# A decoder layer on one core: the third merge gate by seven products, spread over the branch pieces, and x's factor copied before x is scaled

## The chip, the core and the metric

The kernel runs on one core of a Trainium2 chip. Its engines are TensorE (PE in the profile, with PEld for its weight loads), VectorE (DVE), ScalarE (ACT), GpSimd (POOL) and SyncE (SP). Each takes its instructions in the order in which they were written down when the program was built, and waits on semaphores for the others. The metric is device microseconds of one execution.

## The reference, cut to what matters

```python
h = rms_norm(x, norm_g)                                  # x: 256 tokens x 1024
(qa, ka, va, ga, ub, vb, gb, qc, gc, ma, mb, mc) = split_cols(h @ w_in, IN_SPLITS)
out_a = moba_attention(rope(qa), rope(ka), va) * silu(ga)      # 6 heads of 128
out_b = gmlp_spatial_gate(ub, vb, ...) * silu(gb)              # 6 groups of 128
out_c = memory_cross_attention(qc, rms_norm(mem), ...) * silu(gc)   # 4 heads of 128
y = (sigmoid(ma) * (out_a @ w_branch_a)
     + sigmoid(mb) * (out_b @ w_branch_b)
     + sigmoid(mc) * (out_c @ w_branch_c))
return rms_norm(x + y @ w_out, final_norm_g)
```

All numbers are float32. `ma`, `mb` and `mc`, the arguments of the three merge gates, are each a product of the 256 x 1024 tokens with 1024 x 1024 weights.

## The kernel before, in words

**Three passes for one product.** Every float32 operand is split into a high part, rounded to the format that TensorE takes (`hi`, `nh`, `ah`, ...), and a low part, the rest (`lo`, `nl`, `al`, ...). A product is high times high, high times low, low times high, summed in PSUM: `mm3`, lines 391 to 394. The activations are split once. The weights stream from memory and are split on the way: ACT copies a piece to its high part (`split_hi`, line 232), DVE subtracts for the low part (`split_lo`, line 236).

**Chunks.** The weights come in pieces of 1 MB, 128 rows of 2048 numbers, and a piece is two chunks. The list `chunks` is the program's spine; it is made from `PLAN`, and the main loop goes over it with index `c`. In each round the loop runs the small units that are due, splits chunk `c + LEAD` (LEAD is 3), asks for a later piece, and writes down the matmuls of chunk `c`. There are three buffers for raw pieces and four pairs of `hi` and `lo`. A `fea` chunk gives 128 columns of one projection for all tokens (16 matmuls, line 548). A `tok` chunk gives 512 columns for two of the eight blocks of 128 input rows (12 matmuls, lines 392 to 394). A `br` chunk takes two blocks of 128 rows of the branch weights; the first eight of them make the left half of y, the next eight the right half, each in the order of the branches a, a, a, b, b, b, c, c. An `out` chunk belongs to the last projection.

**Gates by seven products.** The first two merge gates (0 for branch a, 1 for branch b) go by Strassen's scheme in Winograd's form: tokens and input rows are halved, sums of the blocks are formed, and seven block products stand for eight. The tokens' sums are the tile `s` (`sums`, line 444), made once and kept in the slot named `x2`. The weights' sums are formed by DMA: a block is loaded into one of two buffers, `form_510` (slot `f0`) and `form_636` (slot `mr`), and further blocks are added to it by accumulating DMAs, which POOL issues (lines 212 and 215). In the order 1, 2, 5, 3, 6, 7, 4 the first buffer serves products 1, 5, 6 and 4, the second 2, 3 and 7. A product is a piece of two `st` chunks of six matmuls (`mm_st`, line 484). Its result goes to the tile of the gate in part by ACT copies (line 491) and DVE additions (lines 495, 498 and 500). Product 4 runs on in the PSUM bank of product 7, so its first matmul waits for DVE's subtraction c22, line 500. The third gate (2, for branch c) is plain: eight `tok` chunks named `sig`, after everything else of the input projection.

**What sets the order.** The helper `Units` holds all work beside the streaming: attention, norms, joins, gates. Each unit has an engine, an estimated duration, units that must come first, and a due chunk. It writes a unit down when the estimate says that it fits, and at the due chunk in any case. The order on each engine is thus fixed at build time. A chunk's join is an ACT copy (line 556) and a DVE addition (558); `jt` is its tile for the gates. SiLU of branch b's gate (line 597) is followed on POOL by u times that (598) and by the mixed result times that (988); the product is split for the branch matmul (`obh` on ACT at line 958, `obl` on DVE at 962). The sigmoids are at line 503. The last lines before the output are `y_units`: y is transposed on PE and split.

**The head.** The norm of x needs the tokens' factor. PE spreads it over the partitions in PSUM (`rms_bcast`, line 352), DVE multiplies the first four blocks of x by it from there (`norm_k`, line 642), and POOL the other four from a copy in SBUF, `bc`, that ACT makes (`rms_out`, line 357); ACT first scales those four blocks by the norm's gain (`norm_gain`, line 646). DVE's first multiplication waits for the copy `bc`, since both read the same PSUM bank.

Of the kernel before, what the change touches and what calls it, by code (L numbers as in the profile page):

```python
# [46 lines left out]
FAST = 2  # L47


def plan():  # L50
# [16 lines left out]

TOK = ("vvb", "mv", "sig")
# [66 lines left out]
def tile_hybrid_layer(ctx: ExitStack, tc: tile.TileContext, mw, xT, mem, x, fin_g, ln_g, w, ws, w_sp, b_sp, rope, out):  # L135
# [272 lines left out]
    def mm_tok(c):  # L408
# [22 lines left out]
        elif k0 + 2 == KD and name == "sig":  # L431
            g = o // 512
            if g == 4:
                slot_tile("sigc", [128, 2, 2, 512], "p1")
            sig[g] = V["sigc"][:, g - 4]

            for t in range(2):
                nc.scalar.activation(sig[g][:, t, :], acc[name, o][t], AF.Sigmoid)
                U.run(ACT, 0.62, U.end[f"c{c}"])
# [24 lines left out]
    def mm_st(c):  # L464
# [23 lines left out]
        c11, c21, c12, c22 = (sig[2 * g + o][:, t, :] for o in range(2) for t in range(2))  # L488
# [12 lines left out]
        if i == 4:  # L501
# [471 lines left out]
    sig2 = chunks.index(("tok", "sig", 2048, 6))  # L973
    last_st = max(c for c in range(n_in) if chunks[c][0] == "st")
    U.add("oaTa", None, 0, lambda: pair("a", "x2", HA), after=[f"c{last_st}"])
    for i in range(3):
# [3 lines left out]
        two_split(f"oaT{i}", lambda hs=hs: (V["qk"][:, hs, 0, :], V["ah"][:, hs, :], V["al"][:, hs, :]),  # L980
                  [f"ga_{i}", "oaTa"], due=sig2 - 2)
# [13 lines left out]
    for i in range(3):  # L995
        hs = slice(2 * i, 2 * i + 2)
        two_split(f"obT{i}", lambda hs=hs: (V["ub"][:, hs, :], V["obh"][:, hs, :], V["obl"][:, hs, :]),
                  [f"mg{i}", "obTa"])
    for i in range(2):
# [4 lines left out]
                  [f"gc_{i}", "ocTa"])  # L1004
    U.add("fin", None, 0, load_fin, after=["oaT0", "oaT1", "oaT2"], wait=8.0)
# [4 lines left out]
    def y_units(half, i, after):  # L1010
# [102 lines left out]
    for c in range(n_in):  # L1113
# [160 lines left out]
```

## Time and profile before

| what | us |
|---|---|
| median of 3 runs | 324.89 (324.81 to 325.85) |
| the profiled execution, its own time | 325.81 |
| its span, first to last instruction | 324.1 |

| engine | busy us | share of the span |
|---|---|---|
| PE | 314.0 | 97% |
| PEld | 266.8 | 82% |
| DVE | 246.7 | 76% |
| ACT | 212.5 | 66% |
| POOL | 50.1 | 15% |

The profiled execution is 0.92 us longer than the median, and 1.7 us of its time lie outside the span. Matmuls are pipelined, so two that follow each other overlap in the records: what one costs is the distance between starts. TensorE's granted clock is full, 0.998 on average.

### The profile page before, as it was taken

What the parts mean: (1) busy time and instruction counts of PE and PEld (TensorE: products, weight loads), DVE (VectorE), ACT (ScalarE), POOL (GpSimd) and SP (SyncE); (2) the same over time, 40 slices, a digit from 0 to 9 for tenths busy, and PEclk for the clock granted to TensorE, in tenths of its full rate; (3) what the DMA queues carried; (4) which work ended last, traced back from release to release, by engine and by line L of the source; (5) the groups of instructions that cost most, each with busy time, mean ns of one, the idle gap of its engine ahead of it and who ended that gap; (6) DMA issues with size and microseconds to landing.
All of it is one profiled execution on the core that took longest, in us unless ns stands there. A gap on an engine that the chain in (4) does not pass through costs nothing.

```text
span 324.1 us, 4506 instructions
## 1 busy us (share of the span) xinstructions
PE 314.0 (97%) x1638; PEld 266.8 (82%) x1638; DVE 246.7 (76%) x353; ACT 212.5 (66%) x354; POOL 50.1 (15%) x50
## 2 busy tenths in 40 slices
PE   8998999999999999999999999998999999999992
PEld 4886888889888888888888888887888888888982
DVE  3979989597579678869687899879775559769452
ACT  4868785564988566786787796567995633434433
POOL 1004730001001110000300441644310000000022
PEclk9999999999999999999999999999999999999999
DMA  7999796845469899488589789823658466463003
GB/s 247 407 421 358 302 330 242 370 138 163 90 229 261 151 232 302 146 257 325 166 169 358 155 229 250 238 113 129 215 203 290 145 235 275 161 230 130 0 8 124
DMA packets 14422, 71.21 MB, mean 220 GB/s; under 512 B 1856, under 2 KB 3008, under 8 KB 8128
## 3 DMA queue, kind: packets, MB, share of 16 engines
q1 hardware_dynamic: 12960, 62.21, 53.1%
q0 software_dynamic: 1152, 8.39, 13.9%
q10 hardware_dynamic: 288, 0.33, 0.3%
q8 instruction: 13, 0.21, 0.3%
q14 instruction: 9, 0.07, 0.1%
HBM read 69.08 MB, written 1.05 MB: 216 GB/s over the span
## 4 chain that ended last, share of the span: by engine, by line
PE 85%; DMA 7%; ACT 4%; DVE 3%; issue 0%; ACTq 0%; SPq 0%
PE acc L548 31%; PE acc L393 11%; PE acc L394 11%; PE acc L392 11%; PE acc L484 10%; DMA st<-in_mw_dram 3%; DMA xt<-in_xT_dram 3%; PE aux L393 2%; PE aux L394 2%; PE aux L392 2%; DVE lo L236 2%; PE aux L718 2%; ACT hi L232 1%; PE aux L942 1%; DVE n L400 1%; DVE xt L642 1%
## 5 line engine op out<-in xcount | busy, mean ns | idle before, releaser
L236 DVE TENSOR_TENSOR lo<-raw,hi 128x1024 fp32r<-128x1024 f32 x86 | 113.6, 1327 | 41.4 <-ACT hi L232 40.2
L232 ACT ACTIVATE hi<-raw 128x1024 fp32r<-128x1024 f32 x86 | 90.5, 1058 | 37.1 <-PE acc L394 30.8
L548 PE MATMUL acc<-n,hi 128*128 128x512 f32 x304 | 79.9, 393 | 0.0
L548 PEld LDWEIGHTS acc<-n,hi 128*128 128x128 f32 x304 | 55.4, 189 | 9.6
L548 PEld LDWEIGHTS acc<-n,lo 128*128 128x128 f32 x304 | 41.4, 190 | 3.8 <-DVE lo L236 0.8
L548 PE MATMUL acc<-n,lo 128*128 128x256 f32 x304 | 42.5, 282 | 0.4 <-DVE lo L236 0.4
L236 DVE TENSOR_TENSOR lo<-form,hi 128x1024 fp32r<-128x1024 f32 x28 | 35.5, 1280 | 6.0 <-ACT hi L232 6.0
L393 PE MATMUL acc<-lo,n 128*128 128x512 f32 x80 | 31.2, 391 | 1.3 <-DVE lo L236 1.3
L392 PE MATMUL acc<-hi,n 128*128 128x512 f32 x80 | 31.3, 391 | 0.1
L394 PE MATMUL acc<-hi,n 128*128 128x512 f32 x80 | 31.1, 389 | 0.0
L232 ACT ACTIVATE hi<-form 128x1024 fp32r<-128x1024 f32 x28 | 29.2, 1051 | 0.5 <-PE acc L484 0.5
L215 POOL DMA_DIRECT2D form<-in_ws_dram x8 | 7.1, 884 | 135.0 <-DVE lo L236 129.9
L484 PE MATMUL acc<-hi,s 128*128 128x512 f32 x64 | 21.9, 397 | 0.0
L393 PEld LDWEIGHTS acc<-lo,n 128*128 128x128 f32 x80 | 15.0, 188 | 4.6 <-DVE lo L236 1.6
L392 PEld LDWEIGHTS acc<-hi,n 128*128 128x128 f32 x80 | 15.0, 188 | 3.5 <-ACT hi L232 0.4
L394 PEld LDWEIGHTS acc<-hi,n 128*128 128x128 f32 x80 | 15.0, 188 | 3.1
L484 PE MATMUL acc<-hi,n 128*128 128x512 f32 x48 | 16.6, 399 | 1.0 <-ACT obh L958 1.0
L1087 POOL TENSOR_TENSOR xk<-xk,fing 128x512 f32<-128x512 f32 (+1 forms) x4 | 4.0, 1013 | 78.9 <-ACT jk L1083 78.9
L484 PEld LDWEIGHTS acc<-hi,s 128*128 128x128 f32 x64 | 12.0, 188 | 2.3
L484 PE MATMUL acc<-lo,s 128*128 128x512 f32 x32 | 12.5, 391 | 0.0
L556 ACT ACTIVATE qk<-acc 128x256 f32<-128x256 f32 x12 | 4.6, 386 | 11.7 <-PE acc L548 11.7
L556 ACT ACTIVATE jt<-acc 128x256 f32<-128x256 f32 x14 | 5.3, 380 | 10.4 <-PE acc L548 10.3
(227 smaller groups left out, 579.3 us busy)
## 6 DMA issues: line engine op xcount, KB each, us to landing
raw<-in_w_dram SPq DMA_DIRECT2D x34, 1024.0 KB, 4.8
raw<-in_w_dram SPq DMA_DIRECT2D x18, 512.0 KB, 7.8
form<-in_ws_dram POOLq DMA_DIRECT2D x8, 1024.0 KB, 8.4
form<-in_ws_dram SPq DMA_DIRECT2D x6, 1024.0 KB, 5.5
st<-in_mw_dram SPq DMA_DIRECT2D x6, 384.0 KB, 7.1
xk<-in_x_dram SPq DMA_DIRECT2D x2, 512.0 KB, 8.9
xt<-in_xT_dram SPq DMA_DIRECT2D x2, 512.0 KB, 10.1
mm<-in_mem_dram SPq DMA_DIRECT2D x2, 512.0 KB, 11.9
```

The source lines that it names most:

```text
L215: nc.gpsimd.dma_start(form_tile(i), block(g, b), accum_op=OP.add)
L232: nc.scalar.activation(hi[c][:, a:b], raw[c // 2][:, o + a:o + b], AF.Copy)
L236: nc.vector.tensor_tensor(lo[c][:, a:b], raw[c // 2][:, o + a:o + b], hi[c][:, a:b].bitcast(F32), OP.subtract)
L392: nc.tensor.matmul(p, s_hi, m_hi, start=first, stop=False)
L393: nc.tensor.matmul(p, s_hi, m_lo, start=False, stop=False)
L394: nc.tensor.matmul(p, s_lo, m_hi, start=False, stop=last)
L400: nc.vector.tensor_tensor(dl, p, dh.bitcast(F32), OP.subtract)
L484: nc.tensor.matmul(p, x[:, k0 + k, tsl(t)], wt[c][:, a * 512:(a + 1) * 512], start=first and a + j == 0, stop=half == 1 and a + j == 3, sk ...
L548: nc.tensor.matmul(o, wt, m, start=i == 0, stop=i == len(passes) - 1)
L556: nc.scalar.activation(dst, pa, AF.Copy)
L718: nc.tensor.transpose(p[:, hsl(j)], src, ident)
L1087: nc.gpsimd.tensor_tensor(z, z, V["fing"][:, a:b], OP.mult)
```

## The change

- `FAST` is 3: the third gate goes by seven products as well. Its eight `tok` chunks are gone, and 14 `st` chunks come in; its weights lie in memory as blocks for this scheme, with the left and right half of the columns exchanged.
- The first two gates' products are placed so that every two of the last `fea` chunks are followed by one product: the sixth and the seventh product of gate 1 each move ahead by two `fea` chunks.
- The third gate's seven products and the eight branch pieces (two chunks each) are dealt in turn: product, piece, product, piece, and so on, the pieces in the order left a, left a and b, left b, right a, right a and b, right b, and at last left c, right c without a product between.
- The third gate's products use the other four PSUM banks (`aux`); the branch sums keep `acc`. The tokens' sums and the normed tokens must stay until the last product, so branch a's parts `ah` and `al` go to other slots and are split earlier, and y's tile is made after product 4.
- The sigmoids are due when their branch piece needs them, the table of square roots is loaded after the last branch chunk, and the final gain is loaded after the last use of `ah`.
- In the head, `norm_gain` waits for `xrms`, the copy `bc`.

```diff
-FAST = 2
+FAST = 3
...
+    late = st[15:]
+    del st[15:]
...
-                 "ub4", "", "ga0", "", "ga2", "", "ga4", "", "gb0", "gb2", "", "gb4", ""):
+                 "ub4", "", "ga0", "", "ga2", "", "ga4", "", "gb0", "", "gb2", "", "gb4", ""):
...
-    return p + [("sig", g) for g in range(2 * FAST, 6)]
+    br = [("br", (h, i)) for h, i in ((0, 0), (0, 1), (0, 2), (1, 0), (1, 1), (1, 2), (0, 3), (1, 3))]
+    for piece, n in zip(br, (1, 1, 1, 1, 1, 1, 0, 0)):
+        p += [piece] + late[:n]
+        del late[:n]
+    return p
...
-            acc[key] = acc_bank()
+            acc[key] = acc_bank() if g < 2 else bank()
...
+        def gate(o, after, due):
+            y = sig[2 * g + o]
+            U.add(f"sgm{g}{o}", ACT, 1.1, lambda: nc.scalar.activation(y, y, AF.Sigmoid), after=["silu"] + after, due=due)
+
+        if g == 2 and i == 7:
+            gate(0, ["c122", "c222"], at_br[0, 7])
+        elif g == 2 and i == 4:
+            gate(1, ["c112", "p24"], at_br[1, 7])
+            pair("y", "n2", KD)
+        elif i == 4:
             for o in range(2):
-                U.add(f"sgm{g}{o}", ACT, 1.1, lambda o=o: nc.scalar.activation(sig[2 * g + o], sig[2 * g + o], AF.Sigmoid),
-                      after=["silu", f"c11{g}", f"c12{g}", f"c22{g}", f"p{g}4"], due=n_in - 8 + 2 * g + o)
+                gate(o, [f"c11{g}", f"c12{g}", f"c22{g}", f"p{g}4"], at_br[o, 2 + 3 * g] - o)
...
-            U.add(f"ng{k}", ACT, 0.42, lambda k=k: norm_gain(k), after=["load_xt"], due=5)
+            U.add(f"ng{k}", ACT, 0.42, lambda k=k: norm_gain(k), after=["load_xt", "xrms"], due=6)
...
-    U.add("oaTa", None, 0, lambda: pair("a", "x2", HA), after=[f"c{last_st}"])
+    def alloc_a():
+        slot_tile("ah", [128, HA, S], "ga", F32R)
+        low = slot_tile("al0", [128, 4, S], "gc", F32R), slot_tile("al1", [128, 2, S], "v1", F32R)
+        V["al"] = [low[0][:, 0:2, :], low[0][:, 2:4, :], low[1]]
...
-                  [f"ga_{i}", "oaTa"], due=sig2 - 2)
+                  [f"ga_{i}", "oaTa"], due=at_br[0, i] - 2)
...
-    U.add("fin", None, 0, load_fin, after=["oaT0", "oaT1", "oaT2"], wait=8.0)
+    U.add("fin", None, 0, load_fin, after=[f"c{at_br[1, 2]}"], wait=8.0)
...
-        if half == 0 and part == 0:
-            nc.scalar.preload_act_table(AF.Sqrt)
-            pair("y", "n2", KD)
...
-                    y_units(half, i, [f"y{c}"])
+                    y_units(half, i, [f"y{c}", f"c{last_st}"])
```

The changed file's line numbers are a few higher or lower for the same code: its `split_hi` is line 238, `split_lo` 242, the product's matmul 482, the join 562 and 564.

**In the head, ACT.** The rows after the second pair of weight splits, before and then changed; `jt` is a join of the memory's keys, `xt` the tokens, `bc` the copy of the factor, `n` the normed tokens' high part.

```order
L232 ACTIVATE hi<-raw 128x1024 x2
L556 ACTIVATE jt<-acc 128x256
L646 ACTIVATE xt<-xt,gains 128x256 x4
L357 ACTIVATE bc<-aux 128x256
L651 ACTIVATE n<-xt 128x2x256 x2
```

```order
L238 ACTIVATE hi<-raw 128x1024 x2
L562 ACTIVATE jt<-acc 128x256
L363 ACTIVATE bc<-aux 128x256
L652 ACTIVATE xt<-xt,gains 128x256 x4
L657 ACTIVATE n<-xt 128x2x256 x2
```

The copy `bc` stands ahead of the four scalings.

**Ahead of product 4 of gate 1, DVE.** The rows that end with the subtraction c22 for which product 4's first matmul waits (line 500, then 498; `sigb` and `sigs_1726` are the same gate's tile). `form_510` is the first weight buffer, here with product 4's sum; `al` is branch a's low part.

```order
L558 TENSOR_TENSOR jt<-jt,acc 128x256
L236 TENSOR_TENSOR lo<-raw,hi 128x1024
L962 TENSOR_TENSOR obl<-ub,obh 128x512
L236 TENSOR_TENSOR lo<-form_510,hi 128x1024 x2
L558 TENSOR_TENSOR jt<-jt,acc 128x256
L500 TENSOR_TENSOR sigb<-sigb,acc 128x512
```

```order
L242 TENSOR_TENSOR lo<-raw,hi 128x1024
L564 TENSOR_TENSOR jt<-jt,acc 128x256
L968 TENSOR_TENSOR al_2200<-qk,ah 128x512
L242 TENSOR_TENSOR lo<-raw,hi 128x1024
L242 TENSOR_TENSOR lo<-form_510,hi 128x1024 x2
L564 TENSOR_TENSOR jt<-jt,acc 128x256
L498 TENSOR_TENSOR sigs_1726<-sigs_1726,acc 128x512
```

A low part of branch a has come in where one of branch b's stood, and the rows belong to earlier chunks: before, the join ahead of the subtraction is that of the fifth of the six `gb` chunks, now that of the third.

**Around the first sigmoids, ACT.** Before, these are the rows from the copy of gate 1's last product on. In the changed kernel they are those from the copy of the third gate's product 1 on, while PE goes through product 1, the first branch piece and product 2; there `form_636` and `form_510` are products 2 and 5, the first `raw` row is the second piece's first chunk, the one behind the sigmoids its second chunk.

```order
L491 ACTIVATE sigb<-acc 128x512
L958 ACTIVATE a<-qk 128x2x256 x3
L232 ACTIVATE hi<-raw 128x1024
L597 ACTIVATE jt<-jt 128x512
L232 ACTIVATE hi<-raw 128x1024
L503 ACT_TABLE_LOAD
L503 ACTIVATE sig_858<-sig_858 128x1024
L503 ACTIVATE sig_859<-sig_859 128x1024
L503 ACTIVATE sigb<-sigb 128x1024
L232 ACTIVATE hi<-raw 128x1024
```

```order
L489 ACTIVATE sigs_2389<-aux 128x512
L603 ACTIVATE jt<-jt 128x512
L238 ACTIVATE hi<-form_636 128x1024
L238 ACTIVATE hi<-raw 128x1024
L964 ACTIVATE obh<-ub 128x512
L501 ACT_TABLE_LOAD
L501 ACTIVATE sig_858<-sig_858 128x1024
L501 ACTIVATE sig_859<-sig_859 128x1024
L501 ACTIVATE sigs_1726<-sigs_1726 128x1024
L238 ACTIVATE hi<-raw 128x1024
L238 ACTIVATE hi<-form_510 128x1024 x2
```

The last high part of branch b, `obh`, which waits for POOL, now stands right ahead of the table load and three sigmoids, and a branch chunk's split behind them.

## Rows read from the trace of the kernel before

**Rows 1.** The page's engine table: busy time, share of the span, instructions.

```profile
PE 314.0 (97%) x1638; PEld 266.8 (82%) x1638; DVE 246.7 (76%) x353; ACT 212.5 (66%) x354; POOL 50.1 (15%) x50
```

**Rows 2.** The waits of PE's matmuls: who waited for whom, us in total, times, longest.

```profile
PE acc L393 <- DVE lo L236: 1.3, 1, 1.3
PE acc L484 <- ACT obh L958: 1.0, 1, 1.0
PE acc L548 <- DVE lo L236: 0.4, 1, 0.4
```

**Rows 3.** The third gate's plain product: the group of its first passes from 228.4 to 250.2 us (those of lines 393 and 394 have the same count), then from PE's timeline its first matmul and the first of the branches (start us, us).

```profile
L392 PE MATMUL acc<-hi,n 128*128 128x512 f32 x32 | 12.4, 389 | 0.0
...
228.40 0.39 PE L392 MATMUL acc<-hi,n 128*128 128x512 f32 x1
...
250.16 0.39 PE L392 MATMUL acc<-hi,a 128*128 128x512 f32 x1
```

**Rows 4.** PE's timeline over one product of 12 matmuls (product 7 of gate 1): its first row, and the first row behind it.

```profile
216.10 0.40 PE L484 MATMUL acc<-hi,s 128*128 128x512 f32 x1
...
218.84 1.75 PE L548 MATMUL acc<-n,hi 128*128 128x512 f32 x7
```

**Rows 5.** The timeline of the head, all engines (start us, us, engine, line; in brackets the idle time before and its releaser).

```profile
21.15 0.36 ACT L556 ACTIVATE jt<-acc 128x256 f32<-128x256 f32 x1
21.23 0.40 PE L352 MATMUL aux<-dg,ones 128*128 128x256 f32 x2
22.66 1.71 ACT L646 ACTIVATE xt<-xt,gains 128x256 f32<-128x256 f32 x4 [1.14 <-DMA xt<-in_xT_dram]
22.96 0.41 DVE L558 TENSOR_TENSOR jt<-jt,acc 128x256 f32<-128x256 f32 x1
24.27 0.36 ACT L357 ACTIVATE bc<-aux 128x256 f32<-128x256 f32 x1
24.67 1.66 DVE L642 SCALAR_TENSOR_TENSOR xt<-xt,gains,aux 128x256 f32<-128x256 f32 x4 [1.30 <-ACT bc L357]
26.90 0.36 ACT L556 ACTIVATE jt<-acc 128x256 f32<-128x256 f32 x1
27.16 1.99 ACT L232 ACTIVATE hi<-raw 128x1024 fp32r<-128x1024 f32 x2
28.80 2.35 DVE L236 TENSOR_TENSOR lo<-raw,hi 128x1024 fp32r<-128x1024 f32 x2
30.06 0.50 PE L393 MATMUL acc<-lo,n 128*128 128x512 f32 x1 [1.30 <-DVE lo L236]
```

**Rows 6.** The timeline ahead of product 4 of gate 1: POOL, DVE and PE.

```profile
219.60 1.58 POOL L598 TENSOR_TENSOR ub<-ub,jt 128x512 f32<-128x512 f32 x1 [1.26 <-ACT jt L597]
221.26 2.17 POOL L988 TENSOR_TENSOR ub<-ub,mt 128x512 f32<-128x512 f32 x1
...
220.50 4.01 DVE L236 TENSOR_TENSOR lo<-form,hi 128x1024 fp32r<-128x1024 f32 x2 [0.48 <-ACT hi L232]
224.44 0.41 DVE L558 TENSOR_TENSOR jt<-jt,acc 128x256 f32<-128x256 f32 x1
224.77 0.67 DVE L500 TENSOR_TENSOR sigb<-sigb,acc 128x512 f32<-128x512 f32 x1
...
225.59 0.47 PE L484 MATMUL acc<-hi,n 128*128 128x512 f32 x1 [1.02 <-ACT obh L958]
```

**Rows 7.** The timeline of ACT and POOL around the sigmoids.

```profile
228.60 0.60 ACT L491 ACTIVATE sigb<-acc 128x512 f32<-128x512 f32 x1 [0.29 <-PE acc L484]
231.60 0.62 ACT L597 ACTIVATE jt<-jt 128x512 f32<-128x512 f32 x1
...
232.30 1.81 POOL L598 TENSOR_TENSOR ub<-ub,jt 128x512 f32<-128x512 f32 x1 [8.87 <-ACT jt L597]
234.18 1.64 POOL L988 TENSOR_TENSOR ub<-ub,mt 128x512 f32<-128x512 f32 x1
...
233.19 1.28 ACT L503 ACT_TABLE_LOAD   x1
234.48 2.01 ACT L503 ACTIVATE sig<-sig 128x1024 f32<-128x1024 f32 x2
237.35 1.04 ACT L232 ACTIVATE hi<-raw 128x1024 fp32r<-128x1024 f32 x1
```

**Rows 8.** DVE and POOL side by side, where POOL multiplies branch c by its gate.

```profile
190.34 4.42 DVE L236 TENSOR_TENSOR lo<-raw,hi 128x1024 fp32r<-128x1024 f32 x1
...
190.84 2.83 POOL L953 TENSOR_TENSOR mid<-mid,gc 128x512 f32<-128x512 f32 x2
```

**Rows 9.** From the views of lines 212 and 215: time from issue to landing of the loads of a weight block (six, issued by SP), and below of the accumulating ones (eight, issued by POOL).

```profile
DMA to landing us min/median/max: 4.8/5.5/8.3
...
DMA to landing us min/median/max: 8.2/8.4/10.9
```

**Rows 10.** Busy time of each engine (instructions) in two stretches: the third gate's plain product, and the branches.

```profile
228.40:250.20 21.80, 21.80 (x98) 18.06 (x97) 15.71 (x14) 17.68 (x22) 3.44 (x2) 1.00 0.71 242
250.20:293.70 43.50, 43.50 (x197) 36.09 (x196) 29.98 (x34) 20.32 (x23) 0.00 (x0) 1.00 0.57 205
```

More of the change, by code (lines that the diff above doesn't have):

```diff
@@ L174, in tile_hybrid_layer @@
             chunks += [("tok", name, g * 512, 2 * i) for i in range(4)]
-        elif name == "st":
-            chunks += [("st", *g, i) for i in range(2)]
+        elif name in ("st", "br"):
+            if name == "br" and ("br", 0, 0) not in chunks:
+                n_in = len(chunks)
+            chunks += [("st", *g, i) if name == "st" else ("br", g[0], 2 * g[1] + i) for i in range(2)]
         else:
             chunks.append(("fea", name, g))
-    n_in = len(chunks)
-    for half in range(2):
-        chunks += [("br", half, i) for i in range(KD)]
     n_br = len(chunks)
+    at_br = {k[1:]: i for i, k in enumerate(chunks) if k[0] == "br"}
     for kh in range(2):
@@ L430, in mm_tok @@
             evict_v(c, o)
[L431 to L439, printed above, removed]
         elif k0 + 2 == KD:
@@ L478, in mm_st @@
             else:
-                slot_tile("sigb", [128, 2, 2, 512], "p2")
-                sig[2], sig[3] = (V["sigb"][:, o] for o in range(2))
+                t2 = slot_tile(f"sigs{g}", [128, 2, 2, 512], ("p2", "p1")[g - 1])
+                for o in range(2):
+                    sig[2 * g + o] = t2[:, o]
         for a in range(2):
@@ L487, in mm_st @@
             return
-        c11, c21, c12, c22 = (sig[2 * g + o][:, t, :] for o in range(2) for t in range(2))
+        c11, c21, c12, c22 = (sig[2 * g + o][:, t, :] for o in ((0, 1) if g < 2 else (1, 0)) for t in range(2))
         if i in (1, 5, 6, 4):
@@ L970, in alloc @@
         return fn
-    sig2 = chunks.index(("tok", "sig", 2048, 6))
-    last_st = max(c for c in range(n_in) if chunks[c][0] == "st")
-    U.add("oaTa", None, 0, lambda: pair("a", "x2", HA), after=[f"c{last_st}"])
+    def alloc_a():
+        slot_tile("ah", [128, HA, S], "ga", F32R)
+        low = slot_tile("al0", [128, 4, S], "gc", F32R), slot_tile("al1", [128, 2, S], "v1", F32R)
+        V["al"] = [low[0][:, 0:2, :], low[0][:, 2:4, :], low[1]]
+    U.add("oaTa", None, 0, alloc_a, after=["ga_0", "ga_1", "ga_2", "gc_0", "gc_1", f"av{HA - 1}"])
+    last_st = max(c for c in range(n_br) if chunks[c][0] == "st")
     for i in range(3):
@@ L1019, in turn @@
             U.run(DVE, 0.7, U.run(ACT, 0.62, U.t[PE]))
-        U.add(f"yt{half}{i}", PE, 0.44, turn, after=after)
+        U.add(f"yt{half}{i}", PE, 0.44, turn, after=after, due=10 ** 6 if half else at_br[1, 6])
     def mm_br(c):
         _, half, part = chunks[c]
-        if half == 0 and part == 0:
-            nc.scalar.preload_act_table(AF.Sqrt)
-            pair("y", "n2", KD)
-        src = {"a": (V["ah"], V["al"], HA, 0), "b": (V["obh"], V["obl"], GB, 2),
+        src = {"a": (V["ah"], None, HA, 0), "b": (V["obh"], V["obl"], GB, 2),
                "c": (V["och"], V["ocl"], HC, 4)}
@@ L1035, in mm_br @@
             for t in range(2):
-                mm3(acc[br][t], sh[:, k, tsl(t)], sl[:, k, tsl(t)], hi[c][:, i * 512:(i + 1) * 512],
+                low = sl[:, k, tsl(t)] if sl is not None else V["al"][k // 2][:, k % 2, tsl(t)]
+                mm3(acc[br][t], sh[:, k, tsl(t)], low, hi[c][:, i * 512:(i + 1) * 512],
                     lo[c][:, i * 512:(i + 1) * 512], k == 0, k == n - 1)
@@ L1112, in tile_hybrid_layer @@
     dma, ready, free = {}, {}, [13, 19]
-    for c in range(n_in):
+    for c in range(n_br):
         if chunks[c][0] == "st" and chunks[c][3] == 0:
@@ L1228 @@
             continue
-        if name in TOK:
+        if name == "br":
+            parts.append(br[g].reshape(-1))
+        elif name in TOK:
             parts.append(tok(cols[name][:, g * 512:(g + 1) * 512]))
```

18 lines of the change are left out of this document (9 added, 9 removed).

## The prediction, made before the changed kernel had run

> **What bounds the kernel now.** I read the engine table first: PE is busy 314.0 of 324.1 us, DVE 246.7 [rows 1]. A busy PE is not yet the bound, so I read next what its matmuls waited for: three waits above noise, 1.3, 1.0 and 0.4 us [rows 2]. PE is therefore the bound from the head on; a matmul less saves its time, and everything else counts only where it makes PE wait. The timelines at the first two waits [rows 5, 6] and the order of the instructions then show what comes late there, and what will.
>
> **The change part by part.**
>
> *Matmuls.* The plain product is 3 x 32 = 96 matmuls, from 228.40 to 250.16: 21.76 us, 0.227 each [rows 3]. Seven products are 84. Twelve such matmuls took 218.84 - 216.10 = 2.74, or 0.228 each [rows 4], so 84 take 19.18. Saved: 2.6 us, all on PE. The lower bound is nothing less, since no matmul is added elsewhere.
>
> *Splits.* 14 half-size steps stand for 8 chunks, so ACT gets six more copies of 1.04 [rows 7] and DVE six more subtractions of 2.35 / 2 = 1.18 [rows 5], plus three additions of about 0.67 [rows 6]; two of the four eviction copies replace sigmoids of the same size. For DVE this is 9 us more over the two stretches, in which it now works 15.7 + 30.0 of 65.3 us [rows 10]; 55 of 62.7 is 87%. That is cover while chunks are split three ahead of PE. It ends where ACT or DVE stands still for longer than the lead, which the last item looks for. I cost the splits themselves at nothing.
>
> *Head.* Now DVE's first scaling waits until 24.67 for `bc`, which stands behind ACT's four scalings, which wait for x until 22.66 [rows 5]. PE's spread is over at 21.63, ACT's join at 21.51, so in the new order `bc` is done near 22.0. DVE is free at 22.96 + 0.41 = 23.37 and starts 1.3 earlier. Not all of this reaches PE. The subtraction that PE waits for (28.80) needs the high part, which ACT starts at 27.16 behind a join at 26.90 that is tied to PE; its first copy ends near 28.2. So the subtraction starts at 28.2 and PE goes on at about 29.45 for 30.06: 0.6 saved. Bounds: 0 (another wait ends there) and 1.3 (the whole wait). I take 0.6, since the 27.16 is a row.
>
> *Ahead of product 4 of gate 1.* PE waited 1.02 there, until DVE's c22 was done at 224.77 + 0.67 = 225.44 [rows 6]; the profile names ACT, but the matmul waits for c22 and for a high part. In the new order the product comes after two `gb` chunks as before, and DVE's list ahead of c22 is other. Count from the end of the second `gb` chunk, g. ACT's split for the third chunk comes first, then DVE's: subtraction done at g + 1.6, join 2.0, low part of branch a 2.6, three subtractions 3.8, 4.9, 6.0, join 6.4, c22 at g + 7.1, if POOL were silent. But POOL's two multiplications fall into it (SiLU of the first pair is done near g + 2.7). In [rows 6] two subtractions beside such a pair took 4.01 instead of 2 x 1.18, 1.7 more; so c22 ends near g + 8.8. PE arrives at g + 2.74 + 2 x 2.8 = g + 8.3 (two `fea` chunks behind the product). The wait shrinks from 1.0 to about 0.5: 0.5 saved. Bounds: 1.0 saved (POOL costs nothing), 0.9 lost (POOL's whole pair, as [rows 8] would have it, 3.2).
>
> *The sigmoids (a new wait).* Let E be the end of product 1 of the third gate on PE. ACT's list from there: eviction copy at E + 0.2, SiLU of the last pair until E + 1.3, and POOL's two multiplications from E + 1.4. From SiLU's start to the second one's end it was 235.82 - 231.60 = 4.22 [rows 7], so they end at E + 4.9. ACT meanwhile splits two chunks and then stands at `obh`, which waits for POOL: E + 5.0 to 5.6. Behind it stand the table load (1.28), three sigmoids (2.01 for two, so 1.0 each) and only then the copy for the second chunk of the second branch piece: it starts near E + 9.8, ends at 10.8, and DVE's subtraction at 12.1. PE needs that low part at E + 5.45 (a piece) + 2.74 (product 2) + 2.72 + 0.23 = E + 11.1. PE waits about 1.0; with ACT up to 0.7 late from the weight block before, 1.7. I take 1.2; bounds 0 (sigmoids and POOL each a little faster) and 2.0. Queued behind the copy on ACT are product 5's two splits and one more sigmoid, which PE reaches after E + 13.6; by the same count they are ready in time, and DVE regains its lead in the next piece.
>
> *At nothing.* The adding DMAs: from one use of the first buffer to the next lie 13.65 us of PE (a piece, a product, a piece), the add lands in 8.4, at most 10.9 [rows 9]. The adds stand in POOL's queue, but the gate's multiplications behind them wait later for ACT. On SP the final gain waits for branch a's last matmul; the raw loads behind it wait for splits of later chunks anyway. Transposes of y: DVE's four operations need 2.7 us and a branch chunk lies between. The table of square roots (1.28) sits on ACT two chunks before its splits are needed. Both ends are unchanged.
>
> Sum: -2.6 - 0.6 - 0.5 + 1.2 = -2.5 us. The profiled execution took 325.81, which would become 323.3; the median is 0.92 below it, 324.89, so 322.4.
>
> **A rule of the Trainium skill against it.** In [rows 8] one subtraction lasted 4.42 beside 2.83 of POOL, 3.2 more than its 1.18, almost as if it had stood still; in [rows 6] it lost 1.7 beside 3.83. SBUF — State Buffer, "Who interferes with whom", says that VectorE with two inputs in SBUF and GpSimd reading SBUF exclude each other: whoever comes second stands still until the first is done. The first row agrees, the second only half. By the rule DVE would lose the whole of POOL's pair each time; what that gives is the second rival.
>
> **Rivals.**
> 1. *The waits vanish.* The head gives its whole 1.3, c22 is early (1.0 saved), and the sigmoids end before PE needs the copy: -2.6 - 1.3 - 1.0 = -4.9, 320.0. For it: each of the three misses by about 1 us or less. Against: all three must turn out well.
> 2. *POOL holds DVE out.* The wait ahead of product 4 grows to 1.9 (POOL's pair costs 3.2 as in [rows 8]; 0.9 lost) and the new wait to 1.55 (POOL's own pair took 3.83 in [rows 6] against 3.5): -2.6 - 0.6 + 0.9 + 1.55 = -0.75, 324.1, not to be told from before. For it: [rows 8]. Against: [rows 6], where the same kinds of instruction met.
> 3. *The first block of the third gate comes late: slower.* The first buffer is free when product 4 of gate 1 is split, near g + 7.8 with POOL's share, and product 1 of the third gate follows only two `fea` chunks behind product 4 (before, the nearest such reload had four). After landing it takes 2.4 us to a low part; PE arrives at g + 8.8 + 2.74 + 5.6 = g + 17.1, or 17.3 for the low part. The load may take 6.8 us; six loads took 4.8 to 8.3, median 5.5 [rows 9]. At 8.3 PE waits 1.5, and the change still gains 1.0. From 9.3 it gains nothing; at 10.9, the slowest time of the adds, PE waits 4.1: +1.6, 326.5.
> 4. *The product does not do what it says*, that is, DVE at 87% and not PE sets the pace in the branches. The time would be near 324 as well; I count it with rival 2.
>
> **How the numbers follow.** My forecast, 321.4 to 323.4 by the two small terms, has 0.66; rival 1 0.13; rivals 2 and 4 0.14; rival 3 0.07. The bounds of the unknown costs give 320.0 (all at the good end) to 324.89 - 2.6 + 0.9 + 2.0 = 325.2. I leave out half of rival 1 and rival 3: 320.3 to 324.4. A measurement of this kernel tells about 0.3%, 1.0 us, from no change. Faster is the forecast and rival 1: 0.79; the same is rivals 2 and 4: 0.14; slower is rival 3: 0.07.
>
> **What would show it.** Matmuls of the seven-product line: 252 of them, 0.228 apart; the lines of three passes 96 fewer. In the head `bc` near 22.0, DVE's scaling near 23.4, PE's first low pass near 29.4. Ahead of product 4 of gate 1 a wait of 0.5, released by DVE's c22. In the second branch piece, at its second chunk, PE waits about 1 us for a subtraction whose copy stands behind three sigmoids and a table load. If this wait is missing, the sigmoid term was wrong; if PE waits at product 1 of the third gate or ACT stands there for a DMA, it is rival 3; if many short waits for DVE line up through the branches, it is rival 4.

## The result and the profile after

The changed kernel took 321.62 us (median of 4 runs, 321.49 to 322.15); the kernel before, run beside it, 324.85 (324.56 to 325.85). The ratio is 0.9898 with a 95% interval of 0.9874 to 0.9922: 3.2 us faster, where the prediction said 322.4 and so 2.5 faster. The profiled execution took 321.63, with a span of 319.9 against 324.1: 4.2 less, since the profiled execution of before lay 0.9 above its median.

The engine table, which answers to [rows 1], and PE's waits (us in total, times, longest), which answer to [rows 2]:

```profile
PE 310.6 (97%) x1626; PEld 263.9 (82%) x1626; DVE 251.9 (79%) x362; ACT 220.9 (69%) x362; POOL 54.8 (17%) x54
```

```profile
PE aux L428 <- ACT hi L385: 1.0, 2, 0.8
...
PE acc L482 <- DVE sigs L498: 0.7, 1, 0.7
PE acc L399 <- DVE lo L242: 0.7, 2, 0.5
```

PE has 12 matmuls fewer and ACT and DVE 8 and 9 instructions more, as the splits were counted. In [rows 2] the head's wait was 1.3; it is the small one of the two on line 399 now. The other one on that line, and product 4's on line 482, are the two places that the prediction named. Those on line 428 lie before 8.5 us, long before x comes.

The head's timeline (start us, us, engine, line; in brackets the idle time before and its releaser), beside [rows 5]:

```profile
21.80 0.39 ACT L363 ACTIVATE bc<-aux 128x256 f32<-128x256 f32 x1 [0.19 <-PE aux L358]
22.77 1.71 ACT L652 ACTIVATE xt<-xt,gains 128x256 f32<-128x256 f32 x4 [0.59 <-DMA xt<-in_xT_dram]
25.60 0.37 ACT L562 ACTIVATE jt<-acc 128x256 f32<-128x256 f32 x1
25.87 2.00 ACT L238 ACTIVATE hi<-raw 128x1024 fp32r<-128x1024 f32 x2
...
28.72 0.50 PE L399 MATMUL acc<-lo,n 128*128 128x512 f32 x1 [0.19 <-DVE lo L242]
```

The copy `bc` is done at 22.2, before x comes, and everything behind it moved as one piece: the join from 26.90 to 25.60, the weight copies from 27.16 to 25.87, PE's first low pass from 30.06 to 28.72. That is 1.34, where the prediction had 0.6. What held the join before is shown by the two rows of ACT just ahead of it in the kernel before:

```profile
25.58 0.63 ACT L651 ACTIVATE n<-xt 128x512 fp32r<-128x512 f32 x1 [0.94 <-DVE xt L642]
...
26.36 0.64 ACT L651 ACTIVATE n<-xt 128x512 fp32r<-128x512 f32 x1 [0.15 <-DVE xt L642]
```

Two copies of the normed tokens waited for DVE; the join at 26.90 follows the second without a wait of its own.

Ahead of product 4 of gate 1, beside [rows 6]:

```profile
211.16 2.15 POOL L604 TENSOR_TENSOR ub<-ub,jt 128x512 f32<-128x512 f32 x1 [5.46 <-ACT jt L603]
213.39 2.15 POOL L998 TENSOR_TENSOR ub<-ub,mt 128x512 f32<-128x512 f32 x1
...
212.07 4.55 DVE L242 TENSOR_TENSOR lo<-form,hi 128x1024 fp32r<-128x1024 f32 x2
216.88 0.67 DVE L498 TENSOR_TENSOR sigs<-sigs,acc 128x512 f32<-128x512 f32 x1
...
216.61 0.39 PE L554 MATMUL acc<-n,hi 128*128 128x512 f32 x1
217.70 0.47 PE L482 MATMUL acc<-hi,n 128*128 128x512 f32 x1 [0.70 <-DVE sigs L498]
```

The two subtractions beside POOL's pair took 4.55, c22 ended at 217.55, and PE, there at 217.00, waited 0.70.

Around the first sigmoids, beside [rows 7], with the second branch piece on PE:

```profile
231.79 1.62 POOL L998 TENSOR_TENSOR ub<-ub,mt 128x512 f32<-128x512 f32 x1
...
233.44 0.63 ACT L964 ACTIVATE obh<-ub 128x512 fp32r<-128x512 f32 x1 [0.56 <-POOL ub L998]
234.07 1.28 ACT L501 ACT_TABLE_LOAD   x1
235.37 2.01 ACT L501 ACTIVATE sig<-sig 128x1024 f32<-128x1024 f32 x2
237.28 1.04 ACT L501 ACTIVATE sigs<-sigs 128x1024 f32<-128x1024 f32 x1
238.23 1.05 ACT L238 ACTIVATE hi<-raw 128x1024 fp32r<-128x1024 f32 x1
...
239.31 1.23 DVE L242 TENSOR_TENSOR lo<-raw,hi 128x1024 fp32r<-128x1024 f32 x1 [2.48 <-ACT hi L238]
...
239.73 0.39 PE L398 MATMUL acc<-hi,obh 128*128 128x512 f32 x1
240.59 0.50 PE L399 MATMUL acc<-lo,obh 128*128 128x512 f32 x1 [0.47 <-DVE lo L242]
```

The chain is the foretold one: POOL, `obh`, table, three sigmoids, the copy, the subtraction, PE. The wait is 0.47, not 1.2.

A wait costs PE more than the idle time in its row, since matmuls that don't wait overlap and start 0.23 apart. From start to start it was 1.09 ahead of product 4 (216.61 to 217.70) and 0.86 here, and the next matmul came another 0.1 late: 0.9 and 0.7 us for the 0.70 and 0.47 in the rows.

The seven-product line on PE, beside [rows 4], over product 2 of the third gate:

```profile
234.29 0.39 PE L482 MATMUL aux<-hi,n 128*128 128x512 f32 x1
...
237.01 0.39 PE L398 MATMUL acc<-hi,ah 128*128 128x512 f32 x1
```

Twelve matmuls took 2.72, 0.227 each. The terms as these rows have them, waits counted from start to start: matmuls -2.6, head -1.34, product 4's wait -0.3, the new wait +0.7, and the wait of 0.4 on line 548 [rows 2], which is absent here, -0.6 (start to start 0.80 for 0.23). Their sum, -4.1, is the difference of the two spans to 0.1. The last term isn't the change's (see the end), and without it the sum is -3.5.

### The profile page after: what moved, and what is told of

Read it like the earlier page. It is cut to its first block, busy times and chain, and to the rows that moved or that the text cites. A ratio compares the mean times of both kernels' runs of the same rounds, so it can differ in the third digit from the quotient of the medians.

```text
span 319.9 us, 4510 instructions
## 1 busy us (share of the span) xinstructions
PE 310.6 (97%) x1626; PEld 263.9 (82%) x1626; DVE 251.9 (79%) x362; ACT 220.9 (69%) x362; POOL 54.8 (17%) x54
## 3 DMA queue, kind: packets, MB, share of 16 engines
HBM read 72.23 MB, written 1.05 MB: 229 GB/s over the span
## 4 chain that ended last, share of the span: by engine, by line
PE 82%; DMA 5%; DVE 5%; ACT 3%; issue 3%; POOL 1%; SPq 0%; ACTq 0%; DVEq 0%
PE acc L554 31%; PE acc L482 11%; PE acc L399 8%; PE acc L400 8%; PE acc L398 8%; PE aux L482 5%; DMA xk<-in_x_dram 3%; PE aux L399 2%; PE aux L398 2%; PE aux L400 2%; DVE lo L242 2%; DMA st<-in_mw_dram 2%; PE aux L724 2%; PE aux L948 1%; ACT hi L238 1%
## 5 line engine op out<-in xcount | busy, mean ns | idle before, releaser
L242 DVE TENSOR_TENSOR lo<-raw,hi 128x1024 fp32r<-128x1024 f32 x78 | 99.2, 1283 | 32.1 <-ACT hi L238 30.8
L238 ACT ACTIVATE hi<-raw 128x1024 fp32r<-128x1024 f32 x78 | 82.0, 1058 | 24.4 <-PE acc L400 18.4
L242 DVE TENSOR_TENSOR lo<-form,hi 128x1024 fp32r<-128x1024 f32 x42 | 55.5, 1336 | 9.6 <-ACT hi L238 9.3
L238 ACT ACTIVATE hi<-form 128x1024 fp32r<-128x1024 f32 x42 | 43.9, 1053 | 4.2 <-DMA form<-in_ws_dram 1.9
L221 POOL DMA_DIRECT2D form<-in_ws_dram x12 | 10.6, 883 | 158.4 <-DVE lo L242 152.6
L399 PE MATMUL acc<-lo,n 128*128 128x512 f32 x48 | 18.8, 392 | 0.2 <-DVE lo L242 0.2
L398 PE MATMUL acc<-hi,n 128*128 128x512 f32 x48 | 18.7, 390 | 0.0
L400 PE MATMUL acc<-hi,n 128*128 128x512 f32 x48 | 18.7, 389 | 0.0
L482 PE MATMUL acc<-hi,n 128*128 128x512 f32 x48 | 16.6, 400 | 0.7 <-DVE sigs L498 0.7
L482 PEld LDWEIGHTS acc<-hi,n 128*128 128x128 f32 x48 | 9.0, 188 | 2.7 <-ACT jt L562 1.0
L399 PEld LDWEIGHTS acc<-lo,n 128*128 128x128 f32 x48 | 9.0, 188 | 2.4 <-DVE lo L242 0.6
L400 PEld LDWEIGHTS acc<-hi,n 128*128 128x128 f32 x48 | 9.0, 188 | 1.9
```

The costliest lines, as they stand in the source:

```text
L221: nc.gpsimd.dma_start(form_tile(i), block(g, b), accum_op=OP.add)
L238: nc.scalar.activation(hi[c][:, a:b], raw[c // 2][:, o + a:o + b], AF.Copy)
L242: nc.vector.tensor_tensor(lo[c][:, a:b], raw[c // 2][:, o + a:o + b], hi[c][:, a:b].bitcast(F32), OP.subtract)
L398: nc.tensor.matmul(p, s_hi, m_hi, start=first, stop=False)
L399: nc.tensor.matmul(p, s_hi, m_lo, start=False, stop=False)
L400: nc.tensor.matmul(p, s_lo, m_hi, start=False, stop=last)
```

## The experiments

Ratios are to the kernel before, run beside each; its medians were 325.60 (25 runs) beside e1 to e4, 325.42 (11) beside e5 to e8, 325.49 (17) beside e9 to e11 and 325.15 (9) beside e12. Between these series the kernel before itself moved by up to 0.75 us (324.85 beside the result), so medians of different series are compared no closer than that; the rows carry the readings.

**The head's edit undone** (e1), in the changed kernel:

```diff
-... norm_gain(k), after=["load_xt", "xrms"], due=6)
+... norm_gain(k), after=["load_xt"], due=5)
```

> The changed kernel with the head's edit alone undone: the copy bc stands behind the four scalings again. By the prediction's term (0.6 us) the time is 321.6 + 0.6 = 322.2; PE's first low pass starts at about 29.3 to 29.4 instead of 28.72. By the trace of the changed kernel, where the join ahead of the weight split moved with its engine's queue, the head gave its whole 1.3: 322.9, and the first low pass starts near 30.06 again. By a third reading (what the head gives is lost to a later wait) the time stays 321.6.

323.35 us, ratio 0.9934 (0.9909 to 0.9959). PE's first low pass starts at 29.92, and the wait ahead of it is back at 1.32.

**The head's edit alone** (e2), the same lines the other way in the kernel before.

> The kernel before with the head's edit alone. By the prediction's term 324.85 - 0.6 = 324.25; by the trace of the changed kernel 324.85 - 1.3 = 323.5, with PE's first low pass near 28.7 and the wait of 1.3 gone from PE's waits. If a later wait eats it, 324.85.

324.12 us, ratio 0.9950 (0.9931 to 0.9969). The low pass starts at 28.80, still behind a wait of 0.76, because ACT's weight copy now stood for its weights:

```profile
26.43 1.06 ACT L232 ACTIVATE hi<-raw 128x1024 fp32r<-128x1024 f32 x1 [0.82 <-DMA raw<-in_w_dram]
```

Both runs fall on the side of 1.3. x comes at another time in each execution, so the head is best read from the start of ACT's scaling of x to the first low pass, and the rest from there to the end of the span:

| execution | x scaled | first low pass | between | span | from low pass to end |
|---|---|---|---|---|---|
| before | 22.66 | 30.06 | 7.40 | 324.1 | 294.0 |
| e1, head undone | 22.49 | 29.92 | 7.43 | 321.8 | 291.9 |
| e2, head alone | 22.41 | 28.80 | 6.39 | 322.9 | 294.1 |
| e3, order alone | 21.96 | 29.39 | 7.43 | 322.2 | 292.8 |
| e4, sigmoids spread | 22.74 | 28.70 | 5.96 | 319.8 | 291.1 |
| e7, head and order | 22.42 | 28.37 | 5.95 | 321.2 | 292.8 |
| changed | 22.77 | 28.72 | 5.95 | 319.9 | 291.2 |
| changed again (e10) | 22.05 | 28.01 | 5.96 | 319.8 | 291.8 |
| e11, two between | 22.67 | 29.06 | 6.39 | 324.7 | 295.6 |
| e12, two splits moved | 22.86 | 29.05 | 6.19 | 318.7 | 289.6 |

Without the edit the stretch is 7.40 to 7.43, with it 5.95 where the weights are there and 6.19 to 6.39 where ACT stands for them (e2, e11 and e12 here). The edit is worth 1.0 to 1.5.

**Products 7 and 4 moved, alone** (e3), in the kernel before:

```diff
-... "gb0", "gb2", "", "gb4", ""):
+... "gb0", "", "gb2", "", "gb4"):
```

> The kernel before with one line of the plan changed: products 7 and 4 of gate 1 each stand two fea chunks earlier, the third gate stays plain. By the prediction's term the wait ahead of product 4 shrinks from 1.0 to 0.5 and the time is 324.85 - 0.5 = 324.35; by what the changed kernel showed there (0.70) 324.5. If POOL held DVE out for its whole pair, the wait grows to 1.9: 325.7. With head and this place together explained, what is left of the change's gain (3.2) is the 12 matmuls less and the burst of sigmoids.

324.06 us, ratio 0.9960 (0.9936 to 0.9983). This was better than either theory had it: the wait of 1.0 is gone altogether, and the stretch from the low pass to the end is 1.2 shorter.

```profile
213.09 1.84 POOL L598 TENSOR_TENSOR ub<-ub,jt 128x512 f32<-128x512 f32 x1 [6.06 <-ACT jt L597]
...
212.56 1.22 DVE L236 TENSOR_TENSOR lo<-form,hi 128x1024 fp32r<-128x1024 f32 x1
214.00 2.01 DVE L236 TENSOR_TENSOR lo<-form,hi 128x1024 fp32r<-128x1024 f32 x1 [0.22 <-ACT hi L232]
216.32 0.68 DVE L500 TENSOR_TENSOR sigb<-sigb,acc 128x512 f32<-128x512 f32 x1
...
218.16 0.40 PE L484 MATMUL acc<-hi,n 128*128 128x512 f32 x1
```

c22 is done at 217.00, 1.16 ahead of PE. Here POOL's pair starts 0.5 behind the first subtraction, in the changed kernel 0.9 ahead of it; the subtractions took 1.22 and 2.01 instead of 4.55 for the two. So the 0.70 in the changed kernel is not what was left of the old wait: it came anew, with the third gate's order.

**The sigmoids spread** (e4), in the changed kernel:

```diff
-gate(o, [f"c11{g}", f"c12{g}", f"c22{g}", f"p{g}4"], at_br[o, 2 + 3 * g] - o)
+gate(o, [f"c11{g}", f"c12{g}", f"c22{g}", f"p{g}4"] + [f"c{at_br[o, 2 + 3 * g] - o - 3}"] * (g + o > 0), at_br[o, 2 + 3 * g] - o)
```

> The changed kernel; of the three sigmoids in the burst only the one that the second branch piece needs stays, the two others wait until three chunks before their own piece needs them. If the burst makes PE's wait of 0.47 at the second chunk of the second branch piece, ACT comes to that chunk's copy 2 us earlier, the wait is gone and the time is 321.6 - 0.5 = 321.1. If the wait comes from obh's wait for POOL or the table load alone, it stays: 321.6. If the sigmoids are late where they now stand, new waits on DVE or PE appear ahead of the later branch pieces: 322 or more.

321.30 us, ratio 0.9863 (0.9840 to 0.9886). One sigmoid stands ahead of the copy, which starts 1.3 earlier (1.9 counted from product 4, which PE began at 218.35 here), and the low pass of the second piece has no idle time before it:

```profile
236.95 1.05 ACT L238 ACTIVATE hi<-raw 128x1024 fp32r<-128x1024 f32 x1
...
240.57 0.39 PE L399 MATMUL acc<-lo,obh 128*128 128x512 f32 x1
```

The burst made the wait. From the low pass to the end it is worth 0.7 against e10 (291.8 and 291.1 in the table; the wait of 0.4 on line 554 is in both), in the median 0.3 to 0.4 against the changed kernel's 321.62 and 321.66, which is less than the runs tell apart.

**POOL's pair held back** (e5), in the changed kernel, and **both** (e6), with the sigmoids spread as well:

```diff
-after=[f"gb{h - 1}", f"gb{h}", "exps"])
+after=[f"gb{h - 1}", f"gb{h}", "exps"] + [f"c{chunks.index(('st', 1, 4, 1))}"] * (h == 1))
```

> The changed kernel; SiLU and POOL's two multiplications of branch b's first pair are held back until product 4 of gate 1 is written down, so that no POOL work lies beside the subtractions ahead of it. If POOL makes them long, the two subtractions of product 4 take 2.35 us instead of 4.55, c22 comes before PE, the wait of 0.70 is gone and the time is 321.6 - 0.7 = 320.9. If another wait (ACT's high part of product 4) ends there as well, the wait stays near 0.7: 321.6. If the pair held back now meets the splits of the third gate's first product and makes PE wait there, 321.6 to 323.

> The changed kernel with both edits: POOL's first pair held back, and the sigmoids spread. If the two waits (0.70 and 0.47) are independent, both are gone and the time is 321.6 - 1.2 = 320.4. If DVE has no room for both (87% busy there by the prediction's count), one of them comes back elsewhere: 320.9 to 321.6.

e5: 323.22 us, ratio 0.9934 (0.9917 to 0.9952); e6: 321.22, ratio 0.9871 (0.9853 to 0.9890). Of e5, DVE's pair without POOL, and PE in the second branch piece:

```profile
212.84 2.35 DVE L242 TENSOR_TENSOR lo<-form,hi 128x1024 fp32r<-128x1024 f32 x2
```

```profile
237.82 0.50 PE L399 MATMUL acc<-lo,ah 128*128 128x512 f32 x1 [0.61 <-DVE lo L242]
...
241.41 0.50 PE L398 MATMUL acc<-hi,obh 128*128 128x512 f32 x1 [0.81 <-ACT hi L238]
...
242.67 0.50 PE L399 MATMUL acc<-lo,obh 128*128 128x512 f32 x1 [0.76 <-DVE lo L242]
```

The pair takes 2.35 again and product 4 waits for nothing, so POOL was what made it 4.55. But the pair held back pushes the next two later on POOL, `obh` waits for the last, and the burst with all behind it comes later: 2.2 us of waits for the 0.70 saved. With the sigmoids spread only the wait of 0.61 stays, at 237.38. The third expectation of e5 had the right kind of loss at the wrong place.

**The change without its third gate** (e7): the kernel before with e2's and e3's edits.

> The kernel before with the head's edit and the two products moved, the third gate plain: the change without its third gate. By the prediction's terms 324.85 - 0.6 - 0.5 = 323.75, so that the third gate gives the changed kernel 2.6 - 1.2 = 1.4 and the rest was already had; by the traces (head 1.3, and the wait of 1.0 ahead of product 4 gone here but back at 0.7 in the changed kernel) 324.85 - 1.3 - 1.0 = 322.5, and the third gate by seven products gives 2.6 - 0.5 - 0.7 = 1.4 less some noise, near 1: both say that the third gate is worth less than the 2.6 of its matmuls. If the third gate gives its whole 2.6, this kernel is at 324.2.

322.92 us, ratio 0.9927 (0.9912 to 0.9941); the changed kernel's medians in two other series are 321.62 and 321.66. By the medians the third gate by seven products gave 1.3 of the 2.6 us that its matmuls save, by the profiled executions 1.0 (from the low pass to the end 292.8 here and 291.8 in e10, which both have the wait of 0.4 on line 548). The two waits, 0.70 and 0.47 in the rows and 0.9 and 0.7 by the starts, which this kernel has neither of, took the rest.

**Products in a block** (e8) and **two between pieces** (e11), the latter with the sigmoids spread. The third gate's last six products are dealt among the eight branch pieces by one tuple:

```diff
-... (1, 1, 1, 1, 1, 1, 0, 0) ...
+... (6, 0, 0, 0, 0, 0, 0, 0) ...    e8
+... (2, 2, 1, 1, 0, 0, 0, 0) ...    e11
```

In e8 product 4 follows 7 at once, and c22 of the third gate is subtracted when half of product 4 is already in the bank: that quarter of the gate differs, the amount of work doesn't.

> The changed kernel with the third gate's last six products in a row behind the first branch piece, not dealt among the pieces. If the adding transfers are hidden only by the pieces between the products (landing in 8.6 us and 2.3 for the splits, against 13.65 us of PE's work from one use of the first buffer to the next in the changed kernel, and 5.5 here), PE waits about 2.7 ahead of product 6, 1 ahead of 7 and 5.6 ahead of 4: 9 us, so 330. If the transfers are hidden anyway by the splits that run three chunks ahead, the time stays near 321.6.

> The changed kernel with the sigmoids spread and the third gate's products dealt two, two, one, one behind the first four pieces: the stretch from one use of the first buffer to the next falls from 13.65 us of PE to 10.9 between products 5 and 6. An adding load lands in 8.5 us (at most 11.1) and its splits take 2.3 more. If the reload is what needs the pieces, PE waits 0 to 2 us ahead of product 6 and ACT shows waits for DMA ahead of its splits: 321.3 to 323.5. If the loss in the block of six came from the burst of sigmoids and not from the loads, there is no wait: 321.3.

e8: 345.63 us, ratio 1.0626 (1.0599 to 1.0652), a loss of 24 where 9 were expected; e11: 326.53, ratio 1.0032 (1.0012 to 1.0053), 5 above the kernel with the sigmoids spread alone, where at most 2 were. Of e11, ACT standing for product 6's block, and PE behind it:

```profile
250.18 1.06 ACT L238 ACTIVATE hi<-form 128x1024 fp32r<-128x1024 f32 x1 [6.02 <-DMA form<-in_ws_dram]
```

```profile
251.29 0.50 PE L482 MATMUL aux<-hi,s 128*128 128x512 f32 x1 [0.54 <-ACT hi L238]
```

The adding loads landed in 8.8 us (median; 8.6 in the changed kernel); what changed is the time in which they must: product 6's was issued at 241.46, when product 5's last split was done, and ACT could go on at 250.18. So the pieces between the products are what hides them, and at a spacing of 10.9 us an adding load comes too late, as rival 3 feared for the plain one. In e11 PE waits 2.0 at product 6 (0.54, 0.76 and 0.68), the end of what was expected, and 1.1 more at product 5 (0.38 and 0.76), which now follows product 2 at once: ACT stood 2.85 for its load, and its second copy stands behind `obh`, table and sigmoid as well. From start to start these five waits cost 4.6, and the stretch from the low pass to the end is 4.5 longer than e4's; the other 0.4 is the head, where ACT stood for its weights.

Of e8's 17 us of waits, 3.0 are at product 5, behind its load (2.84 on ACT) and the burst; of the others the two long ones, 7.58 and 4.44, follow ACT's standing for adding loads, 7.90 and 4.88. What e8 lost beyond them has a second cause in its windows (columns: stretch, its length, busy us of PE, PEld, DVE, ACT, POOL, clock, DMA share, GB/s):

```profile
236.00:241.50 5.50, 3.24 (x14) 2.23 (x12) 1.55 (x3) 5.49 (x6) 0.00 (x0) 1.00 0.89 369
241.60:258.60 17.00, 8.66 (x20) 6.28 (x20) 7.27 (x7) 6.46 (x8) 2.59 (x3) 0.50 0.74 132
```

The granted clock was full (2.4 GHz) until PE had stood for 2.26 us, and half of it (1.2 GHz) from 241.6 to 258.6; it was half again from 265.5 to 268.8, after a wait of 4.44. Two matmuls that take 0.62 at the full clock took 1.05 there, and three in a row 1.28, 0.427 each for 0.227. For some 27 matmuls that is an estimated 5 us. The waits are 18 by the starts, so the two together make 23 of the 24.

**The branch splits moved** (e9), with the sigmoids spread:

```diff
-[f"ga_{i}", "oaTa"], due=at_br[0, i] - 2)
+[f"ga_{i}", "oaTa", f"c{chunks.index(('fea', 'gb', 2))}"], due=at_br[0, i] - 2)
-[f"gc_{i}", "ocTa"], due=at_br[0, 6] - 2)
+[f"gc_{i}", "ocTa", f"c{chunks.index(('st', 2, 1, 1))}"], due=at_br[0, 6] - 2)
```

> The changed kernel with the sigmoids spread, and with the splits of branches a and c held back (a until the third gb chunk, c until product 1 of the third gate), so that on DVE no branch split and only one of product 4's two subtractions stands ahead of c22. POOL's pair stays where it was. If c22 was late by what stood ahead of it on DVE and by POOL together, c22 comes 1.5 to 2 us earlier, the wait of 0.70 is gone and so is the one of 0.47: 321.6 - 1.2 = 320.4, against 321.3 with the sigmoids spread alone. If the moved splits press on the first branch pieces, waits appear there: 321.3 to 322.

322.62 us, ratio 0.9902 (0.9874 to 0.9930): slower than the kernel with the sigmoids spread alone. c22 ended at 213.56, more than 3 us ahead of PE, but the order on ACT had changed further on: both copies for the second branch piece came behind `obh`, table and sigmoid, and PE waited twice there, 0.76 each time (until 237.58 and 238.84).

```profile
236.48 1.99 ACT L238 ACTIVATE hi<-raw 128x1024 fp32r<-128x1024 f32 x2
```

**The changed kernel again** (e10).

> The changed kernel itself, on the same chip as the kernels beside it. 321.6 as before if chips agree; what it differs by is the error of comparisons across calls.

321.66 us, ratio 0.9870 (0.9839 to 0.9900). The median is that of the result, while the kernel before is 0.6 slower beside it, so the gain is 3.2 in one series and 3.8 in the other.

**Two splits moved** (e12), with the sigmoids spread:

```diff
-[f"ga_{i}", "oaTa"], due=at_br[0, i] - 2)
+[f"ga_{i}", "oaTa"] + [f"c{chunks.index(('fea', 'gb', 2))}"] * (i > 0), due=at_br[0, i] - 2)
```

> The changed kernel with the sigmoids spread, and of branch a's splits only the second and third held back until the third gb chunk, so that SiLU stands one weight copy later on ACT and ACT's order around the first sigmoids stays that of the kernel with the sigmoids spread. If the order is what decides, POOL's first pair meets product 4's subtractions later (as in the kernel before with the two products moved, where c22 came 1.2 us ahead of PE), the wait of 0.70 is gone or under 0.2, the second branch piece stays without a wait: 320.6 to 320.8. If what is taken from DVE's and ACT's list ahead of c22 always comes back at the second branch piece, as in the three kernels before this one, a wait of 0.5 to 1.5 appears there: 321.2 to 322.2.

320.05 us (319.93 to 320.38), ratio 0.9838 (0.9825 to 0.9852): the fastest, 1.6 below the changed kernel's medians, which are of other series. From the low pass to the end the first profile of the changed kernel has 291.2 and this one 289.6, both without the wait of 0.4 on line 554; the two waits that are gone cost 0.9 and 0.7 there. Of PE's waits that ahead of the first low pass is left, and two of 0.8 and 0.3 before 7 us:

```profile
PE acc L399 <- DVE lo L242: 0.5, 1, 0.5
```

The place ahead of product 4:

```profile
212.08 1.84 POOL L604 TENSOR_TENSOR ub<-ub,jt 128x512 f32<-128x512 f32 x1 [6.06 <-ACT jt L603]
...
211.55 1.22 DVE L242 TENSOR_TENSOR lo<-form,hi 128x1024 fp32r<-128x1024 f32 x1
212.99 2.02 DVE L242 TENSOR_TENSOR lo<-form,hi 128x1024 fp32r<-128x1024 f32 x1 [0.22 <-ACT hi L238]
215.31 0.68 DVE L498 TENSOR_TENSOR sigs<-sigs,acc 128x512 f32<-128x512 f32 x1
...
217.15 0.40 PE L482 MATMUL acc<-hi,n 128*128 128x512 f32 x1
```

POOL's pair starts 0.9 later than in the changed kernel, the first subtraction 0.5 earlier, and c22 ends 1.16 ahead of PE, as in e3. At the second branch piece the low part comes just in time. Order decided, not the amount of work: DVE is busy 252.3 us and ACT 220.9, against 251.9 and 220.9 in the changed kernel.

## Why the prediction was right, and where it was wrong

*The bound.* Right: PE from the head on. The profiled spans that were followed here (e4, e7, e10, e11, e12) come out of PE's matmuls, its waits counted from start to start, and the time of x, to 0.2 us.

*Matmuls.* -2.6 by the counts, and 0.227 each in the rows after. But e7 shows that only 1.0 to 1.3 of it reached the end with the rest of the change; the forecast for that split was 1.4.

*Head.* This is the step that failed in size: "behind a join at 26.90 that is tied to PE". The first half of the chain came as foretold (`bc` at 22.2 for 22.0, DVE's scaling at 23.39 for 23.4), and then the prediction held the join where it was. The join was tied to ACT's own queue, which stood for DVE's scalings before it; when those came earlier, so did the join, by 1.3. The term was 0.6; e1 and e2 give 1.0 to 1.5, at the end of its bounds and beyond, since 1.3 was the idle time in a row and not what the wait cost. By the starts, head and new wait were 0.7 and 0.5 too dear and product 4's wait 0.2 too cheap, which makes 1.0: -3.5 for the -2.5 forecast. In the medians the forecast was 0.8 too slow. The two large errors went the same way, so the number isn't right by their cancelling; a range of 2 us either way had room for both.

*Ahead of product 4.* Size nearly right (0.5 forecast, 0.70 waited in the row), by the right mechanism: counted from g = 208.53, c22 was put at g + 8.8 and came at g + 9.0, PE at g + 8.3, where, by the starts, it was ready (216.61 + 0.23). What the count hid is that the wait was avoidable, as e3 and e12 show: with the SiLU one weight copy later on ACT, the 0.70 turns into 1.16 of slack.

*The new wait.* Right place, releaser and cause (e4); 0.47 for 1.2. With E = 228.85, POOL was done at E + 4.56 for E + 4.9 and the copy started at E + 9.4 for 9.8, while PE, by the starts, was ready at E + 11.1 as foretold. The chain was 0.4 shorter, and the allowance of 0.2 for a late ACT wasn't needed: 0.6 of delay, of which the row shows 0.47 as idle.

*At nothing.* The adding DMAs: right, and e8 and e11 show how near it was: at 13.65 us of spacing no wait of PE, at 10.9 already 2.0.

*The rivals.* Rival 1 had the head right and the two waits wrong. Rival 3: ACT did wait 1.87 for the first block of the third gate, but PE didn't. Rival 4: no string of short waits in the branches. Rival 2 went wrong in an instructive way. The rule of the Trainium skill (SBUF — State Buffer, "Who interferes with whom") that VectorE with two inputs in SBUF and GpSimd reading SBUF exclude each other holds here to about 0.1 us (last section). The prediction misread its price. It took POOL's recorded times as the time for which POOL keeps DVE out. They contain POOL's own standing still for DVE.

## What to carry to other kernels

A row shows that an instruction started late, not what it was tied to: before a gain is cut short at such a row, ask what released it, and whether that moves too. What a wait costs is read from the starts of the matmuls around it, not from the idle time in the row. Work that waits for a slow engine (here a copy that waits for POOL) should have nothing behind it that PE needs soon; look at what the order puts there. When two engines exclude each other, who comes first counts: here POOL's pair starting 0.5 behind DVE's first subtraction instead of 0.9 ahead of it saved PE the whole wait.

## What was not expected of the hardware

*Turns between DVE and POOL.* Of e5, a subtraction beside POOL's two multiplications:

```profile
219.77 2.35 DVE L242 TENSOR_TENSOR lo<-raw,hi 128x1024 fp32r<-128x1024 f32 x1
...
219.74 1.30 POOL L604 TENSOR_TENSOR ub<-ub,jt 128x512 f32<-128x512 f32 x1 [13.24 <-ACT jt L603]
221.12 2.16 POOL L998 TENSOR_TENSOR ub<-ub,mt 128x512 f32<-128x512 f32 x1
```

POOL comes first and ends at 221.04. DVE's record is 2.35 for 1.22 elsewhere and ends at 222.12, 1.08 later. POOL's second starts its record at 221.12 but ends at 223.28, 1.16 behind DVE's end. In the changed kernel's rows the same count holds: POOL's first until 213.31, a subtraction until 214.39 (its own record starts at 212.07 and lasts 2.32), POOL's second until 215.54, the other subtraction until 216.62. So here they take turns by instruction, each record includes the standing, and a multiplication costs DVE about 1.15, not the 2.15 in its row. The 2.2 here is two such turns; the 1.7 of [rows 6] fits two, the first of them half over when DVE came, but no run took that apart. Turns are not the rule everywhere: in [rows 8] both multiplications went ahead of one subtraction.

*A meeting that goes either way.* In [rows 8] a subtraction was held out by both multiplications of branch c, and PE waited 0.40 [rows 2]. The changed kernel has the same instructions there. In its first profile DVE went first; in the second (e10) POOL did, and PE waited 0.41 again, at 192.77:

```profile
189.02 1.23 DVE L242 TENSOR_TENSOR lo<-raw,hi 128x1024 fp32r<-128x1024 f32 x1
...
189.52 4.11 POOL L959 TENSOR_TENSOR mid<-mid,gc 128x512 f32<-128x512 f32 x2
```

```profile
188.27 4.44 DVE L242 TENSOR_TENSOR lo<-raw,hi 128x1024 fp32r<-128x1024 f32 x1
...
188.77 2.85 POOL L959 TENSOR_TENSOR mid<-mid,gc 128x512 f32<-128x512 f32 x2
```

What decides it wasn't tried. The wait is in twelve of the fourteen profiled executions and absent in the first of the changed kernel and in e12's. It is a part of the spread between executions of one kernel, and the -0.6 in the account of the two spans is this and not the change.
